# A fourth prepared half tile in the joint phase, with the forget gate kept in DRAM and one head pair moved behind the phase

## The chip, the cores and the metric

The kernel runs on one core of one Trainium2 chip. The metric is the device time of one execution in microseconds. TensorE (PE) multiplies, VectorE (DVE) and ScalarE (ACT) do elementwise work, GpSimd (POOL) and SyncE (SP) mostly issue DMAs. SBUF is the memory on the chip, PSUM holds the products, DRAM is outside.

## The reference

One layer of a hybrid decoder, 256 tokens of 2048 features, all in float32:

```python
h = rmsnorm(x, pre_norm_g[l])
proj = h @ w_in[l]
(a_q, a_k, a_v, a_g, a_lr, b_q, b_k, b_v, b_g, m_a, m_b) = jnp.split(proj, offsets, axis=-1)
gk = jax.nn.log_sigmoid((a_lr @ gla_gk_w2[l] + gla_gk_b[l])) / 16
o_a = gla_chunked(a_q, a_k, a_v, gk)             # gated linear attention, 4 heads
y_a = (rmsnorm(o_a, gla_norm_g[l]) * jax.nn.silu(a_g)) @ w_branch_a[l]
o_b = diff_attention(b_q, b_k, b_v, lam)         # differential attention, 16 heads
y_b = (rmsnorm(o_b, diff_norm_g[l]) * 0.8 * jax.nn.silu(b_g)) @ w_branch_b[l]
out = (jax.nn.sigmoid(m_a) * y_a + jax.nn.sigmoid(m_b) * y_b) @ w_out[l]
x = x + rmsnorm(out, post_norm_g[l])
```

`gk`, the log of the forget gate, is a 256 x 1024 array. It is made early, from the 16 columns `a_lr`, and read only when the scores of the gated linear attention are computed.

## The kernel before

**Half tiles.** Every weight matrix is streamed from DRAM once. Its unit is a half tile of 128 x 1024 elements. `emit_half` (L339) splits the next one of the list `seq` into a rounded high part (`hi`, written by ACT, L371) and a low part (`lo`, what is left, written by DVE, L372); TensorE then multiplies both with the split activations. `take` (L380) hands half tile j to the product that needs it, and before that calls `emit_half` until half tile j + `AHEAD` (3) is emitted. `hi` and `lo` lie in `wpool`, which has three buffers of each, so the conversion of half tile j + 3 starts when TensorE has finished half tile j.

**Stages.** First come the values of the linear attention (`v0`, `v2`, `v3`), while small tasks, among them `forget_gate` (L644), run beside them. Then comes the joint phase, described next. Behind it stand the remaining query and key heads of the differential attention (`diff_heads`), with the tasks of the attention scores (`gla_scores`, `gla_out`, `diff_lane`) in between, then the branch products, the output product and the final norm.

**The joint phase.** Ten sets of projection columns are multiplied with seven block products instead of eight (`PRODUCTS`, in the order 1, 3, 2, 5, 6, 7, 4). Each product has two tiles t of two half tiles h, so a set has 28 half tiles of six matmuls each. The operands of these products are sums and differences of weight blocks. Loads bring blocks a and b (`link`) and c (L242); DMAs that add while they write (L252, on POOL's queue) and additions on DVE (L260, in `follow_set`) turn them into the next operand in place. `phase_steps` (L102) writes the order out by hand. After both half tiles of a place listed in `PARTNERED` or `MORE_PARTNERS` it puts one half tile of other work, a partner: `v4`, the keys and queries of the linear attention, and the first `EARLY` (3) pairs of heads. A partner has 16 matmuls. Ten sets with six partners and four more make 64 partners. `pinned` keeps the matmuls of the phase in exactly this order.

**Buffers.** The pool behind `u` (L158) has `BIG` = 18 buffers of 128 x 1024. The activations hold eight of them all through the phase, and the forget gate `gp` two. The rest serve the c blocks, the gates `gl` and `gr` that each set makes, and the gathered `q` and `k`. Those are stored to DRAM by `spill` (L174) and come back by `fetch` (L180), both on POOL's queue in program order; in the last set the steps at (7, 1, 0) fetch `q` and `k` of both halves for `gla_scores`, which reads `gp` as `pre` (L948, L967).

**Pace.** Outside the phase, `tick` (L541) counts half tiles and advances the first three score tasks each time `PACE` half tiles have gone by: 1.5 in the stretch of heads ("linear"), 1.75 later.

Of the kernel before, what the change touches and what calls it, by code (L numbers as in the profile page):

```python
# [7 lines left out]
F32R = mybir.dt.float32r  # L8
# [6 lines left out]
P = 128  # L15
# [6 lines left out]
VG = (416, 416, 416, 416, 400)  # L22
RANK = 16
AHEAD = 3
LANES = 3
X_LOADS = {0: (2, 2), 1: (4, 4), 2: (8, 4), 3: (12, 4)}
ROWS = {"two": 2, "tok": 4, "chan": KT}
# [6 lines left out]
LINKS = {(3, 1): ("a", 0), (2, 0): ("a", 1), (7, 1): ("b", 0), (4, 0): ("b", 1)}  # L34
RAWS_AT = ((4, 1, 0), (2, 0, 1), (5, 1, 0))
PAIRS = [(g, pair) for g in range(4) for pair in range(2)]
EARLY = 3
PARTNERED = ((2, 1), (5, 1), (6, 0), (6, 1), (7, 0), (7, 1))
MORE_PARTNERS = ((0, 1, 0), (0, 1, 1), (0, 3, 1), (0, 5, 0))
SPILL_AT = (3, 0, 0)  # L40
PACE = {"linear": 1.5, "pairs": 1.75}
BIG = 18
MORE = 16
BRIDGE = 512
# [57 lines left out]
def phase_steps():  # L102

    keys = ["v4"] + [f"{name}{hf}{c}" for hf in range(2) for name in ("k", "q") for c in range(4)]
    keys += [f"{name}{g}{c}" for g, pair in PAIRS[:EARLY] for name in ("dq", "dk") for c in (2 * pair, 2 * pair + 1)]
    other = [(key, r, h) for key in keys for r in range(4 if key == "v4" else 1) for h in range(2)]
    slots = [(s, prod, t) for s in range(SETS) for prod in PRODUCTS for t in range(2)]
    mixed = []
    for slot in slots:
        mixed += [("set", *slot, h) for h in range(2)]  # L110
        s, prod, t = slot
        for _ in range(((prod, t) in PARTNERED) + (slot in MORE_PARTNERS)):
            mixed.append(other.pop(0))
    return mixed + other

# [27 lines left out]
def hybrid_kernel(ctx: ExitStack, tc, xt, xn, preg, postg, w, w2, gkb, glag, lamv, diffg, ident_d, causal_d, lmask_d, out):  # L143
# [14 lines left out]
    def u(shape, name, dtype=F32):  # L158
        count[0] += 1
        return big.tile(shape, dtype, tag="u", name=f"{name}_{count[0]}")  # L160
# [13 lines left out]
    def spill(t, name):  # L174
        count[0] += 1
        d = dram.tile(list(t.shape), t.dtype, name=f"{name}_{count[0]}")
        tc.keep_in_program_order(pool.dma_start(d, t))
        return d

    def fetch(d, name, make, queue=pool):  # L180
        t = make(list(d.shape), name, d.dtype)
        tc.keep_in_program_order(queue.dma_start(t, d))
        return t
# [23 lines left out]
    seq = halves_of("v0", "v2", "v3") + phase_steps()  # L207
# [3 lines left out]
    emitted = [0]  # L211
# [114 lines left out]

    loaded = [0]
    joint_loads = [False]
    alive = [0]

    def load_next(done):
# [7 lines left out]
    def emit_half():  # L339
        j = emitted[0]  # L340
        emitted[0] += 1
        e = seq[j]
        while loaded[0] < min(j + 2, len(seq)):
            if len(seq[loaded[0]]) == 3 and seq[loaded[0]][2] == 0:
                load(loaded[0])
            loaded[0] += 1
        joined = e[0] == "set"
        for link_ in part_links.get(e, ()):
            part_link(*link_)
        if e[0] == "part":  # L350
            r = chain[e[1], {3: "b", 7: "f"}.get(e[2], "e"), e[3]]
        else:
            r = emit_set(*e[1:]) if joined else emit_plain(j, *e)
        n = r.shape[1]
        if e[0] in ("o2", "o3") and j + 1 < len(seq):
            make = u if e == ("o3", 1, 0) else u2
            hi_t, lo_t = make([P, 1024], "keep", F32R), make([P, 1024], "keep", F32R)
        else:
            hi_t = wpool.tile([P, 1024], F32R, tag="hi", name=f"hi_{j}")
            lo_t = wpool.tile([P, 1024], F32R, tag="lo", name=f"lo_{j}")  # L360
        fine = 2 if j < 2 else 1
        cuts = [(n * i // fine, n * (i + 1) // fine) for i in range(fine)]
        if j == 0:
            prep_x(0)
            a, b = cuts[0]
            tc.keep_in_program_order(dve.tensor_copy(hi_t[:, a:b], r[:, a:b]))
            a, b = cuts[1]
            tc.keep_in_program_order(act.activation(hi_t[:, a:b], r[:, a:b], AF.Copy))
        for a, b in cuts:
            if j:  # L370
                act.activation(hi_t[:, a:b], r[:, a:b], AF.Copy)  # L371
            dve.tensor_tensor(out=lo_t[:, a:b], in0=r[:, a:b], in1=f32(hi_t[:, a:b]), op=ALU.subtract)  # L372
        if joined:
            follow_set(*e[1:])
        part_follow(e)
        ready[j] = (e, hi_t, lo_t)
# [3 lines left out]
    def take(key):  # L380
        j = used[0]
        used[0] += 1
        while emitted[0] < min(j + 1 + AHEAD, len(seq)):
            emit_half()
        e, hi, lo = ready.pop(j)
        assert key in (e, e[0]), (e, key)
        return hi, lo
# [130 lines left out]
    ts, heads = {}, {}  # L518
# [22 lines left out]
    def tick(part):  # L541
# [4 lines left out]
        if beat[0] > pace - 0.01:  # L546
            beat[0] -= pace
            pump(LANES)

# [94 lines left out]
    def forget_gate():  # L644
        w2_raw = w2_tile[0]
        w2_s = lend("s2l", "w2_s", F32R)
        top = lend("r3h", "w2h", F32R)
        r = slice(64, P)
        late = tc.keep_in_program_order
        late(act.activation(w2_s[:64, :], w2_raw[:64, :], AF.Copy))  # L650
        late(act.activation(top[r, :], w2_raw[r, :], AF.Copy))
        late(dve.tensor_tensor(out=w2_s[r, :], in0=w2_raw[r, :], in1=f32(top[r, :]), op=ALU.subtract))
        yield
        bank = ps("bg")
        for b in range(2):
            pe.transpose(bank[:, P * b : P * b + P], lr[:, b, :], ident)
        top = t2([P, 512], "lrh").bitcast(F32R)
        lrt = sm([P, S], "lrt", F32R, bufs=1)
        act.activation(top[:, :S], bank[:, :S], AF.Copy)
        for i in (0, 64):  # L660
            act.activation(lrt[i : i + 32, :], bank[i : i + 32, :S], AF.Copy)
            r = slice(i + 32, i + 64)
            dve.tensor_tensor(out=lrt[r, :], in0=bank[r, :S], in1=f32(top[r, :S]), op=ALU.subtract)
        yield
        gp.extend(u([P, 2, 4, P], "gp") for _ in range(2))
        for hf in range(2):
            for c in range(2):
                bank = ps("bg")
                for i in range(2):
                    ct = 4 * hf + 2 * c + i  # L670
                    o = bank[:, S * i : S * i + S]
                    pe.matmul(o, w2_s[:, P * ct : P * ct + P], lrt, start=True, stop=True)
                for i in range(2):
                    ct = 4 * hf + 2 * c + i
                    act.activation(gp[hf][:, :, 2 * c + i, :], bank[:, S * i : S * i + S].rearrange("p (b t) -> p b t", b=2), AF.Identity, bias=gkb_s[:, ct : ct + 1])
            yield
        e = [lend(tag, "e") for tag in ("r3h", "r3l")]
        z = [t.rearrange("p b c t -> p (b c t)") for t in gp]
        for hf in range(2):
            act.activation(e[hf], z[hf], AF.Abs)  # L680
            yield
            act.activation(e[hf], e[hf], AF.Exp, scale=-1.0)
            yield
        for hf in range(2):
            act.activation(e[hf], e[hf], AF.Ln, bias=1.0)
            yield
            dve.scalar_tensor_tensor(out=z[hf], in0=z[hf], scalar=0.0, in1=e[hf], op0=ALU.min, op1=ALU.subtract)
        done.add("gate")

    gp = []  # L690
# [229 lines left out]
    sets = (step for s in range(SETS) for step in block_products(s))  # L920
    rest = others()
    pinned[0] = joint_loads[0] = True
    fetched = []
    for n, step in enumerate(phase_steps()):
        if n == PUT_OFF:
            put_off.pop()()
        if step == ("set", SETS - 1, 7, 1, 0):
            fetched = [[fetch(ts[name, hf], name, u) for name in ("q", "k")] for hf in range(2)]
        next(sets if step[0] == "set" else rest)
    for gen in (sets, rest):  # L930
        assert next(gen, DONE) is DONE
    pinned[0] = joint_loads[0] = False
    joint.close()
    more = ctx.enter_context(tc.tile_pool(name="more", bufs=MORE))
    pools[:] = ctx.enter_context(tc.tile_pool(name="small", bufs=2)), more
# [390 lines left out]
    while "out" not in done:  # L1326
        pump(LANES)
    parts_a = []
# [7 lines left out]
    for g in range(4):  # L1336
        parts_a.append(fetch(m0[g], "part", u))
        banks = token_major(f"y0{g}", 512, a_ops, LANES, 4 if g == 3 else 8)
        if g < 3:
# [4 lines left out]
    def settle(q):  # L1344
        while not {("pair", q // 2, pair) for pair in range(2)} <= done:
            pump(LANES)

# [93 lines left out]
    def half_operand(ops, to, prod, kt):  # L1441
# [4 lines left out]
        while name not in to:  # L1446
            pump(LANES)
        return [t[:, kt, :] for t in to[name]]
# [93 lines left out]
    for n, step in enumerate(branch_steps()):  # L1542
# [3 lines left out]
        if n % 3 == 2 or {"lane0", "lane1"} <= done:  # L1546
            pump(LANES if len(tasks) > 1 else 1)
    pinned[0] = False
# [27 lines left out]
    for g in (2, 3):  # L1576
# [7 lines left out]
        if g == 2:  # L1584
            total(0, 2, bank, 2)
            for b in range(2):
                xres.append([])
                for i in range(2):
                    t = u([P, 1024], "xres")
# [3 lines left out]
    t = total(0, 3, bank)  # L1593
# [10 lines left out]
    for c in range(2):  # L1604
        bank = held["x"][:, 256:] if c else ps("mm")[:, :256]
        for kt in range(8, KT):
            lo = 512 * (kt % 2) + 256 * c
# [3 lines left out]
        if c == 0:  # L1611
            t = cell(1, 3)[:, :256]
# [4 lines left out]
        else:  # L1617
            end = ps("bg")
            c = slice(TURNED[0] % 1024, TURNED[0] % 1024 + 512)
            t = yg[1, 1][:, c]  # L1620
# [67 lines left out]
```

## Time and profile before

| | |
|---|---|
| median of 3 runs | 1079.25 us (1079.2 to 1079.81) |
| profiled execution | 1080.03 us |
| its span in the profile | 1078.1 us |
| PE busy | 1066.4 us (99%) |
| weight loads busy | 914.4 us (85%) |
| DVE busy | 959.7 us (89%) |
| ACT busy | 765.3 us (71%) |
| POOL busy | 179.6 us (17%) |
| DMA | 295.54 MB, mean 274 GB/s |
| joint phase | about 84 to 639 us |

Matmuls overlap, so the busy time of PE is longer than the sum of their pitches would be; the distance between the starts of successive matmuls says whether TensorE runs at its rate. A row of the timeline has start, length, engine, line, operation, output and inputs, the count of merged instructions, and in brackets the idle time of the engine before it with what ended it. A row of the waits has total, count and longest.

### The profile page before, as it was taken

To read this page: it belongs to the slowest core of one execution; us is meant where nothing else is said; L and a number is where in the kernel's file an instruction comes from. 1 tells how busy PE (TensorE), PEld (TensorE's weight loads), DVE (VectorE), ACT (ScalarE), POOL (GpSimd) and SP (SyncE) were. 2 spreads that over 40 slices of the span, in tenths; PEclk is the share of its full clock that TensorE was granted. 3 is DMA by queue.
4 is the path that set the end of the run, shared out by engine and by line. 5 is a ranking of instruction groups with operands and counts; after the bars stand their busy time and mean duration, and the time that the engine had idled before them with its cause. 6 is when DMAs were issued, how large, how long until landed. Compare 5 with 4: busy or idle time off the path is not lost.

```text
span 1078.1 us, 15451 instructions
## 1 busy us (share of the span) xinstructions
PE 1066.4 (99%) x5380; PEld 914.4 (85%) x5380; DVE 959.7 (89%) x1273; ACT 765.3 (71%) x1122; POOL 179.6 (17%) x259
## 2 busy tenths in 40 slices
PE   9999999999999999999999999999999999999997
PEld 8998888888888888888888888898988888888886
DVE  7798999999999999999999989976877988889886
ACT  7897676777676767676767766765687887566662
POOL 0201121212121212121212211012111112100000
PEclk9999999999999999999999999999999999999999
DMA  9899798989898989999898867769989888988752
GB/s 349 271 352 310 194 339 259 322 230 320 224 324 215 310 245 335 284 273 303 267 298 262 206 231 279 253 206 310 334 282 305 264 269 273 346 303 257 271 192 99
DMA packets 68365, 295.54 MB, mean 274 GB/s; under 512 B 8832, under 2 KB 11904, under 8 KB 51648
## 3 DMA queue, kind: packets, MB, share of 16 engines
q1 hardware_dynamic: 38080, 167.99, 43.8%
q0 software_dynamic: 29632, 125.84, 42.6%
q8 instruction: 42, 0.69, 0.3%
q10 hardware_dynamic: 576, 0.73, 0.2%
q14 instruction: 35, 0.29, 0.1%
HBM read 267.27 MB, written 27.26 MB: 273 GB/s over the span
## 4 chain that ended last, share of the span: by engine, by line
PE 82%; DVE 7%; issue 5%; ACT 2%; DMA 2%; POOL 1%; POOLq 0%; SPq 0%; DVEq 0%; ACTq 0%
PE mm L579 55%; PE bg L579 20%; DVE lo L372 3%; PE mm L567 2%; PE bg L567 2%; DMA vback<-vl 1%; PE mm L552 1%; DVE a L260 1%; ACT prob L1158 1%; ACT hi L371 1%; DMA raw<-in_w_dram 0%; DVE prob L1152 0%; PE bg L1172 0%; PE bg L1064 0%; PE bg L1364 0%
## 5 line engine op out<-in xcount | busy, mean ns | idle before, releaser
L371 ACT ACTIVATE hi<-raw 128x1024 fp32r<-128x1024 f32 (+3 forms) x213 | 217.0, 1025 | 117.0 <-PE bg L579 51.7
L372 DVE TENSOR_TENSOR lo<-raw,hi 128x1024 fp32r<-128x1024 f32 (+3 forms) x215 | 251.8, 1177 | 39.7 <-ACT hi L371 36.8
L371 ACT ACTIVATE hi<-a 128x1024 fp32r<-128x1024 f32 x160 | 169.3, 1061 | 53.7 <-PE mm L579 35.3
L372 DVE TENSOR_TENSOR lo<-a,hi 128x1024 fp32r<-128x1024 f32 x160 | 190.6, 1220 | 6.3 <-ACT hi L371 4.4
L579 PE MATMUL mm<-hi,xs 128*128 128x512 f32 (+1 forms) x608 | 155.8, 382 | 0.0
L579 PEld LDWEIGHTS mm<-hi,xs 128*128 128x128 f32 x608 | 114.0, 188 | 18.5
L579 PE MATMUL bg<-xs,hi 128*128 128x512 f32 x448 | 115.4, 390 | 0.0
L372 DVE TENSOR_TENSOR lo<-b,hi 128x1024 fp32r<-128x1024 f32 x80 | 97.8, 1223 | 12.3 <-ACT hi L371 9.9
L579 PEld LDWEIGHTS bg<-xs,hi 128*128 128x128 f32 x448 | 84.2, 188 | 16.4
L371 ACT ACTIVATE hi<-b 128x1024 fp32r<-128x1024 f32 x80 | 84.2, 1059 | 19.2 <-PE mm L579 17.3
L579 PE MATMUL mm<-lo,xs 128*128 128x512 f32 (+1 forms) x304 | 88.6, 381 | 0.0
L579 PE MATMUL mm<-xs,hi 128*128 128x512 f32 x320 | 82.2, 394 | 0.0
L252 POOL DMA_DIRECT2D b<-in_w_dram x40 | 34.9, 873 | 204.7 <-DVE a L260 123.1
L579 PEld LDWEIGHTS bg<-xs,lo 128*128 128x128 f32 x448 | 60.9, 190 | 6.9 <-DVE lo L372 2.8
L579 PEld LDWEIGHTS mm<-xs,hi 128*128 128x128 f32 x320 | 57.4, 189 | 9.9
L579 PEld LDWEIGHTS mm<-lo,xs 128*128 128x128 f32 x304 | 57.0, 188 | 9.7
L579 PE MATMUL bg<-xs,lo 128*128 128x256 f32 x448 | 62.8, 283 | 1.5 <-DVE lo L372 1.5
L372 DVE TENSOR_TENSOR lo<-c,hi 128x1024 fp32r<-128x1024 f32 x40 | 49.0, 1226 | 5.5 <-ACT hi L371 1.4
L579 PE MATMUL mm<-hi,oah 128*128 128x512 f32 x128 | 50.9, 397 | 1.3 <-DVE part L1334 1.3
L371 ACT ACTIVATE hi<-c 128x1024 fp32r<-128x1024 f32 x40 | 42.5, 1062 | 11.8 <-PE mm L579 10.9
L579 PE MATMUL mm<-hi,oal 128*128 128x512 f32 x128 | 50.1, 391 | 0.0
L260 DVE TENSOR_TENSOR a<-a,b 128x1024 f32<-128x1024 f32 x40 | 48.8, 1221 | 0.6
(408 smaller groups left out, 2283.9 us busy)
## 6 DMA issues: line engine op xcount, KB each, us to landing
raw<-in_w_dram SPq DMA_DIRECT2D x90, 1024.0 KB, 7.6
c<-in_w_dram SPq DMA_DIRECT2D x40, 512.0 KB, 6.9
a<-in_w_dram POOLq DMA_DIRECT2D x40, 512.0 KB, 9.5
b<-in_w_dram POOLq DMA_DIRECT2D x40, 512.0 KB, 8.3
a<-in_w_dram POOLq DMA_DIRECT2D x18, 1024.0 KB, 15.9
b<-in_w_dram POOLq DMA_DIRECT2D x18, 1024.0 KB, 9.8
raw<-in_w_dram SPq DMA_DIRECT2D x14, 832.0 KB, 7.8
gr<-gr POOLq DMA_DIRECT2D x10, 512.0 KB, 13.3
```

Source lines behind the costliest of these rows:

```text
L252: tc.keep_in_program_order(pool.dma_start(chain[s, name, i][:, c], block(s, 1, i)[:, c], accum_op=ALU.add))
L260: add = dve.tensor_tensor(out=a, in0=a, in1=chain[s, "b", i][:, c] if second else raws[s, i, h], op=ALU.add)
L371: act.activation(hi_t[:, a:b], r[:, a:b], AF.Copy)
L372: dve.tensor_tensor(out=lo_t[:, a:b], in0=r[:, a:b], in1=f32(hi_t[:, a:b]), op=ALU.subtract)
L552: i = pe.matmul(out, lhs, rhs, start=first and n == 0, stop=last and n == len(pairs) - 1, **kw)
L567: i = pe.matmul(banks[g][b][:, :n], a[part][:, P * b : P * b + P], w[:, n * g : n * g + n], start=first, stop=last)
L579: i = pe.matmul(*args, **kw)
L1158: act.activation(prob[m][:, lo:up], prob[m][:, lo:up], AF.Exp, scale=score_scale[:, b : b + 1], bias=mx[:, i : i + 1], accum_out=z[:, i : ...
```

## The change

In the joint phase `take` emits four half tiles ahead instead of three (`PHASE_AHEAD`). The buffers for every fourth half tile of the phase come from the pool of `u`, two each time, and the other three keep using `wpool`. `forget_gate` stores its two tiles to DRAM when it ends, and the last set fetches them back, each behind the `q` and `k` of its half. In the eight sets of `LEAN` the partner behind the second tile of product 2 is left out. The partners are then 56, and `EARLY` is 2: the third pair of heads is computed behind the phase, as one of six pairs there instead of five. The pace of the score tasks in the stretch of heads goes from 1.5 to 1.75 half tiles.

```diff
+PHASE_AHEAD = 4
...
-EARLY = 3
+EARLY = 2
 PARTNERED = ((2, 1), (5, 1), (6, 0), (6, 1), (7, 0), (7, 1))
 MORE_PARTNERS = ((0, 1, 0), (0, 1, 1), (0, 3, 1), (0, 5, 0))
+LEAN = (1, 2, 3, 4, 6, 7, 8, 9)
 SPILL_AT = (3, 0, 0)
-PACE = {"linear": 1.5, "pairs": 1.75}
+PACE = {"linear": 1.75, "pairs": 1.75}
...
-        for _ in range(((prod, t) in PARTNERED) + (slot in MORE_PARTNERS)):
+        for _ in range(((prod, t) in PARTNERED[s in LEAN :]) + (slot in MORE_PARTNERS)):
             mixed.append(other.pop(0))
...
+    joined_stage = [0]
...
+        elif joined_stage[0] and (j - joined_stage[0]) % 4 == 3:
+            hi_t, lo_t = u([P, 1024], "hi", F32R), u([P, 1024], "lo", F32R)
         else:
             hi_t = wpool.tile([P, 1024], F32R, tag="hi", name=f"hi_{j}")
...
-        while emitted[0] < min(j + 1 + AHEAD, len(seq)):
+        while emitted[0] < min(j + 1 + (PHASE_AHEAD if joined_stage[0] else AHEAD), len(seq)):
             emit_half()
...
+        gp[:] = [spill(t, "gp") for t in gp]
         done.add("gate")
...
     pinned[0] = joint_loads[0] = True
+    joined_stage[0] = emitted[0]
...
         if step == ("set", SETS - 1, 7, 1, 0):
-            fetched = [[fetch(ts[name, hf], name, u) for name in ("q", "k")] for hf in range(2)]
+            for hf in range(2):
+                fetched.append([fetch(ts[name, hf], name, u) for name in ("q", "k")])
+                gp[hf] = fetch(gp[hf], "gp", u)
...
     pinned[0] = joint_loads[0] = False
+    joined_stage[0] = 0
```

## The prediction

> **What bounds the kernel now.** I read the engine totals of the page first, then the chain in order of time for the rate of TensorE, then the windows set by set, and last the timelines around the few places where a set is longer than its neighbours.
>
> ```profile
> PE 1066.4 (99%) x5380; PEld 914.4 (85%) x5380; DVE 959.7 (89%) x1273; ACT 765.3 (71%) x1122; POOL 179.6 (17%) x259
> ```
> ```profile
> 138.82 21.78 PE mm L579 x96
> 160.60 2.77 PE bg L579 x16
> ```
> ```profile
> 138.82:193.66 54.84, 54.84 (x266) 46.30 (x265) 52.49 (x52) 39.91 (x43) 10.28 (x14) 1.00 0.94 301
> ...
> 413.02:468.45 55.43, 55.10 (x266) 46.21 (x265) 52.56 (x50) 40.37 (x44) 11.89 (x17) 1.00 0.97 299
> ...
> 523.29:579.05 55.76, 55.10 (x266) 46.22 (x265) 53.56 (x53) 40.79 (x45) 12.55 (x18) 1.00 0.89 263
> ```
> ```profile
> PE bg L579 <- DVE lo L372: 1.5, 3, 0.7
> ```
>
> In the joint phase TensorE runs without a gap: 96 matmuls in 21.78 us are 0.227 us each, so a set's half tile (six of them) takes 1.36 us and a partner's half tile (one row of 16) 2.77 us. A set is 28 of the first and six of the second, 54.84 us (the windows' columns are length, then PE, PEld, DVE, ACT, POOL, clock, DMA share, GB/s). The clock is 1.00 throughout. So the sets that last 55.43 and 55.76 show the loss: 0.59 us in set 6 and 0.92 us in set 8, and the chain of waits says what it is: TensorE stood three times for a low part that VectorE (DVE) had not finished. Set 0 has the third place:
>
> ```profile
> 133.92 0.39 PE L579 MATMUL mm<-hi,r3l 128*128 128x512 f32 x1
> 134.51 0.73 PE L579 MATMUL mm<-lo,r3h 128*128 128x512 f32 x2 [0.20 <-DVE lo L372]
> 135.08 1.78 PE L579 MATMUL bg<-xs,hi 128*128 128x512 f32 x7
> 137.38 1.21 PE L579 MATMUL bg<-xs,lo 128*128 128x256 f32 x8 [0.52 <-DVE lo L372]
> ```
>
> At a pitch of 0.227 the second row was due at 134.15 (0.36 late) and the fourth at 135.08 + 7 x 0.227 = 136.67 (0.71 late): 1.07 us. All that can be won in the phase is therefore 1.07 + 0.59 + 0.92 = 2.58 us, of 1078.1.
>
> **Lookahead, three to four half tiles.** How far DVE is ahead is read by pairing its low parts with the matmuls that first use them, here in set 8.
>
> ```profile
> 537.59 5.31 DVE L372 TENSOR_TENSOR lo<-c,hi 128x1024 fp32r<-128x1024 f32 x4
> ...
> 544.39 1.23 DVE L372 TENSOR_TENSOR lo<-a,hi 128x1024 fp32r<-128x1024 f32 x1
> ...
> 549.19 2.36 DVE L372 TENSOR_TENSOR lo<-a,hi 128x1024 fp32r<-128x1024 f32 x2
> ```
> ```profile
> 544.46 0.62 PE L579 MATMUL mm<-lo,xs 128*128 128x512 f32 x2
> ...
> 548.61 0.62 PE L579 MATMUL mm<-lo,r1h 128*128 128x512 f32 x2
> ...
> 551.33 0.61 PE L579 MATMUL mm<-lo,r1h 128*128 128x512 f32 x2
> ```
>
> The low part that ends at 537.59 + 5.31 = 542.90 is used at 544.46: a lead of 1.56 us. It does not grow in the run of 16 set half tiles, because the next conversion must wait for a buffer. At the first half tile of product 5 the lead is 548.61 - 545.62 = 2.99, since the partner that follows product 2 has put 2.77 us of TensorE work there instead of 1.36. Then the additions of L260 come, and two half tiles later the lead is 0.92 (the pair at 549.19 ends at 551.55, the first of it one pitch of 2.36 - 1.22 = 1.14 earlier, at 550.41). One buffer more adds one half tile, 1.36, to the lead wherever the buffer is what holds DVE back: 2.92 in the run, which is long enough for it: DVE gains 1.36 - 1.14 = 0.22 us on each half tile, 3.5 on 16. Later in each second half of a set it also waits for a buffer, and that idle time is what a fourth buffer lets it use:
>
> ```profile
> 123.60 1.23 DVE L372 TENSOR_TENSOR lo<-b,hi 128x1024 fp32r<-128x1024 f32 x1 [0.86 <-ACT hi L371]
> ```
> ```profile
> 453.38 1.22 DVE L372 TENSOR_TENSOR lo<-b,hi 128x1024 fp32r<-128x1024 f32 x1 [0.66 <-ACT hi L371]
> ```
> ```profile
> 563.65 1.22 DVE L372 TENSOR_TENSOR lo<-b,hi 128x1024 fp32r<-128x1024 f32 x1 [0.62 <-ACT hi L371]
> ```
>
> Set 0 can use 0.86 and the lead it carries in, against 1.07 lost: I take 1.0. Set 6 has 0.66 against 0.59: all of it. Set 8 has 0.62 against 0.92, and it loses a partner's evacuation besides: 0.8. Sum **-2.4 us**; the ends are 0 (DVE gets no earlier) and -2.6.
>
> **Eight sets without the partner of product 2.** Each lean set has 54.84 - 2.77 = 52.07 us of TensorE work. DVE loses one low part (1.14) and about 0.3 of evacuation, so of its idle 54.84 - 52.49 = 2.35 us about 1.05 is left: still less than TensorE's work. The lead at product 5 is then 2.92 from the fourth buffer where it was 2.99 from the partner: -0.07, so **0** by itself, as long as the fourth buffer is there. Without it the lead starts at 1.56, and the same additions, which took 2.99 - 0.92 = 2.07, would stop TensorE for 0.51 in each of eight sets: 4.1 us, the upper end.
>
> **The third early pair after the phase.** Eight half tiles leave the phase (8 x 2.77 = 22.2 us) and come back in the stretch that follows, where two half tiles take 650.11 - 644.52 = 5.59:
>
> ```profile
> 644.52 2.23 PE L579 MATMUL mm<-xs,hi 128*128 128x512 f32 x9
> ...
> 650.11 2.23 PE L579 MATMUL mm<-xs,hi 128*128 128x512 f32 x9
> ```
> ```profile
> 634.00:745.00 111.00, 110.90 (x662) 98.19 (x661) 95.57 (x145) 71.96 (x114) 20.85 (x38) 1.00 0.74 258
> ```
>
> 8 x 2.80 = 22.4, **+0.2**. TensorE is full in that stretch too (110.90 of 111), so nothing is filled up. Its weight loads, head stores and later fetches move with it, into a DMA share of 0.74 from one of 0.94.
>
> **Pace 1.75 instead of 1.5.** Five pairs are 40 half tiles, 40 / 1.5 = 26.7 steps of the score tasks; six are 48 / 1.75 = 27.4. The tasks end at the same place against the branch products, with more time a step. **0**, but where a DVE step then falls against the branch products is open: one bank there now comes late,
>
> ```profile
> 871.79 0.50 PE L579 MATMUL mm<-hi,oah 128*128 128x512 f32 x1 [0.83 <-DVE part L1334]
> ```
>
> and a shift can remove such a stop or make another: -1 to +1.
>
> **Forget gate stored and fetched.** Two stores and two fetches of 512 KB on POOL's queue.
>
> ```profile
> L687 DVE SCALAR_TENSOR_TENSOR gp<-gp,e x2: 1219/1222/1224, 69.7 to 72.9; 128x1024 f32<-128x1024 f32 x2
> L967 ACT ACTIVATE decay<-gp x2: 1044/1052/1059, 649.2 to 650.1; 128x1024 f32<-128x1024 f32 x2
> ```
> ```profile
> 79.92 0.91 POOL L252 DMA_DIRECT2D a<-in_w_dram  x1 [11.32 <-DVE lo L372]
> ```
>
> The gate is ready at 74 and POOL sits idle for 11.32 us up to 79.92, so the stores issue in that gap; what is behind them waits for DVE anyway. The fetches stand in POOL's queue among those of q and k, behind which only the last head and gate stores and gate fetches wait; the gate's reader comes at 649, some 25 us after. **0**; if the cover goes, one transfer of about 10 us would hold the score tasks, not TensorE, which has six pairs of head products to run. DVE's waits are unchanged by it.
>
> **Who holds the eighteen big buffers.** Storing the gate frees two, the fourth half tile takes two. The pool was full before: the queue of SP waits in it.
>
> ```profile
> SPq L242 <- DVE a L260: 166.3, 24, 22.9
> SPq L242 <- DMA gl<-gl: 113.3, 7, 29.6
> ```
> ```profile
> gl<-gl POOLq DMA_DIRECT2D x10, 512.0 KB, 14.0
> ```
>
> Loads waited here, off the path. Now a conversion on ScalarE (ACT) can wait in the same pool, with every later half tile behind it on ACT, DVE behind ACT and TensorE behind DVE. The trace of before cannot show that wait. Its ends are 0, if the pair always takes over the buffers its predecessor frees, and, if it has to wait for a store in flight, 14.0 less a lead of 2.9, 11 us each time. Below zero it cannot go, since the gain of the buffer is booked above. I take 0: the count of two for two is the nearer row, and SP's loads are ordered later in the program than the conversions that would need the buffer.
>
> **Sum.** -2.4 + 0 + 0.2 + 0 + 0 + 0, about -2.3 to -2.4. Against the profiled execution (1080.03 us, its span 1078.1 and 1.9 around it) that is 1077.7; the runs' median is 0.78 below that execution, so **1076.9**.
>
> **Rivals.** *The forecast, 0.50*: the three stops of the phase go, 1075.4 to 1077.1 with what the branch products do.
> *Little comes of it, 0.30*: half of the stops go (set 0 keeps its own, because its evacuations of v4 follow one another), or the branch products get one more stop of 1 us: 1079.25 - 1.2 = 1078.0. For it: DVE at 52 of 55 us gives little room; against it: the idle rows above.
> *The fourth pair comes late, 0.14, slower*: its buffer is held by a load or a store in flight, so the lookahead is three again in lean sets that have lost their partner's cushion: eight times 0.51 is 4.1, 1079.25 + 4.1 = **1083.3**. With the stops of the phase gone as forecast, it decides from 2.4 + 2.2 = 4.6 us of such waits: half a microsecond in each of nine sets, or a single whole flight of a store. For it: SP's 113.3 us; against it: the count.
> *DVE becomes the bound of the lean sets, 0.06, slower*: if the 2.35 us that DVE idles in a set cannot be used, a lean set lasts 54.84 - 1.44 = 53.40 instead of 52.07, 1.33 x 8 = 10.6, **1089.9**. Against it: undisturbed sets last 54.84, which is TensorE's sum (28 x 1.36 + 6 x 2.77), and DVE's 52.49 is less; hence the small chance.
> The Trainium skill, Perfetto Trace Analysis, Identifying the Most-Contended Engine, says that matmul busy time is a bad measure, and to judge TensorE by how busy its weight loads are. By that rule TensorE's 85% stands below DVE's 89%, DVE would be the engine to relieve, taking TensorE work from beside it would not shorten a set, and the time would be the last rival's; the even pitch of 0.227 us in this trace does not agree with the rule.
>
> **How the numbers follow.** From no change a measurement of this kernel can tell about 0.2%, 2.2 us: below 1077.1 is faster, above 1081.4 slower. The forecast's case gives 0.50, the second 0.30 same, the last two 0.20. The likeliest case alone is 1075.4 to 1077.1. For 8 in 10 the range runs from 1075.0 (all 2.6 us and a stop of the branch products gone) to 1083.3.
>
> **What would show it.** Right: all lean sets at 52.07 in the windows, no wait of TensorE for a low part between 84 and 612, the lead at product 5 near 2.9, the phase shorter by 22.2 + 2.4. Wrong: ACT's conversions waiting for a DMA of gl, gr or k; sets of 52.6 and more; a lead of 1.5 at product 5; new stops of the branch products by DVE; the gate's fetch ending the wait of L967.

## The result, and the profile after

| | before | after |
|---|---|---|
| median | 1079.22 us (1079.0 to 1079.81) | 1131.7 us (1128.29 to 1134.95) |
| ratio after to before | | 1.0487 [1.0463, 1.0511] |
| profiled execution, span | 1080.03, 1078.1 us | 1134.95, 1133.1 us |

The change makes the kernel 4.9% slower, where 1076.9 us had been predicted. First the engine totals of the page, and then the joint phase as one window of each kernel (columns: length, then busy time and instructions of PE, PEld, DVE, ACT, POOL, granted clock, DMA share, GB/s); before first, from its first half tile to its last:

```profile
PE 1085.5 (96%) x5380; PEld 921.4 (81%) x5380; DVE 953.1 (84%) x1273; ACT 752.8 (66%) x1122; POOL 179.8 (16%) x263
```
```profile
91.20:630.70 539.50, 537.79 (x2584) 454.27 (x2584) 513.76 (x488) 393.35 (x426) 105.72 (x148) 1.00 0.92 277
```
```profile
91.20:659.90 568.70, 532.55 (x2457) 441.82 (x2456) 493.56 (x472) 371.00 (x412) 104.31 (x145) 0.97 0.86 253
```

TensorE, DVE and ACT execute as many instructions as before. The phase has 127 matmul records fewer, since a pair of heads left it, and takes 29.2 us longer. TensorE is now idle for 36 us of it, and the clock is 0.97. The waits of TensorE in the phase (columns: total, times, longest):

```profile
PE mm L584 <- DVE lo L377: 21.8, 9, 7.4
PE mm L584 <- ACT hi L376: 6.3, 5, 5.0
PE mm L584 <- DVE gr L907: 4.8, 4, 2.6
```

(L376 and L377 are the old L371 and L372, L584 is L579.) What DVE and ACT waited for, in two views of the same stretch:

```profile
DVE lo L377 <- DMA gr<-gr: 29.2, 4, 9.4
DVE lo L377 <- DMA gl<-gl: 5.7, 1, 5.7
```
```profile
ACT hi L376 <- DMA gr<-gr: 8.3, 2, 6.0
```

A conversion reads no `gr`. What it waited for is the buffer: its tile was to lie where the gate of the previous set still lay, and that gate's store was in flight. One such place, on POOL, DVE, ACT and PE in turn:

```profile
381.56 0.85 POOL L179 DMA_DIRECT2D gr<-gr  x1
```
```profile
398.45 1.23 DVE L377 TENSOR_TENSOR lo<-raw,hi 128x1024 fp32r<-128x1024 f32 x1 [9.42 <-DMA gr<-gr]
```
```profile
400.89 1.06 ACT L376 ACTIVATE hi<-a 128x1024 fp32r<-128x1024 f32 x1 [7.68 <-DVE lo L377]
```
```profile
392.40 1.07 PE L584 MATMUL mm<-hi,xs 128*128 128x512 f32 x4
400.86 1.22 PE L584 MATMUL mm<-lo,xs 128*128 128x512 f32 x2 [7.39 <-DVE lo L377]
401.88 3.58 PE L584 MATMUL bg<-xs,hi 128*128 128x512 f32 x8
```

POOL issues the store at 381.56. It lands 16.8 us later, at 398.4, and DVE starts its low part at that moment, after 9.42 idle. DVE's low parts run in program order, so the ones behind it wait too. Those that are ready are used up by then: TensorE stands for 7.39 us, and ACT for 7.68, until DVE gives a buffer back. The five waits of DVE for gates are five stops of TensorE. Each ends 2.1 to 2.5 us after the `gr` of its set has landed, which is the time of two conversions, the one that waited for the buffer and the one behind it. (Late means: the distance of the two starts, less the usual pitch.)

| TensorE last started at | next start late by | `gr`, `gl` landed at |
|---|---|---|
| 221.46 us | 2.34 us | 221.5, 222.8 us |
| 276.95 | 5.90 | 280.6, 281.5 |
| 393.08 | 7.55 | 398.4, 399.5 |
| 457.65 | 4.62 | 460.0, 461.2 |
| 621.02 | 5.20 | 624.3, 625.6 |

Together 25.6 us. Six smaller stops (3.06 at 96.4, 2.73 at 129.3, four of 0.8 to 1.2) are for the most part a late load and late gate additions of L907. The matmuls behind a long stop are slow as well:

```profile
393.00:401.00 8.00, 0.61 (x4) 0.18 (x2) 2.55 (x3) 0.32 (x2) 0.00 (x0) 0.84 0.97 395
401.00:405.50 4.50, 4.50 (x12) 3.53 (x13) 4.47 (x5) 2.59 (x4) 0.90 (x1) 0.52 0.20 20
405.50:412.00 6.50, 6.50 (x34) 5.50 (x33) 5.76 (x6) 4.33 (x5) 1.31 (x2) 1.00 0.72 120
```

For 4.5 us after the stop the granted clock is 0.52, and the eight matmuls at 401.88 have a pitch of (405.29 - 401.88) / 8 = 0.426 us instead of 0.227. Added up over the starts of successive matmuls, this costs 11 us in the phase beyond the stops.

The other side of the exchange is SP's queue, in the same stretch:

```profile
SPq L244 <- DVE a L262: 340.2, 14, 54.8
SPq L244 <- DVE lo L377: 94.6, 3, 46.1
```

Before, the loads of c waited for the stores of `gl` and `gr`, off the path. Now no load does: loads take the buffers that the conversions and additions release, and the conversions are left with those under a store.

### The profile page after: what moved, and what is told of

It reads as the page before. It is cut to its first block, busy times and chain, and to the rows that moved or that the text cites. A ratio compares the mean times of both kernels' runs of the same rounds, so it can differ in the third digit from the quotient of the medians.

```text
span 1133.1 us, 15366 instructions
## 1 busy us (share of the span) xinstructions
PE 1085.5 (96%) x5380; PEld 921.4 (81%) x5380; DVE 953.1 (84%) x1273; ACT 752.8 (66%) x1122; POOL 179.8 (16%) x263
## 5 line engine op out<-in xcount | busy, mean ns | idle before, releaser
L377 DVE TENSOR_TENSOR lo<-raw,hi 128x1024 fp32r<-128x1024 f32 (+3 forms) x215 | 251.8, 1179 | 57.0 <-ACT hi L376 43.2
L376 ACT ACTIVATE hi<-raw 128x1024 fp32r<-128x1024 f32 (+3 forms) x213 | 215.4, 1022 | 89.1 <-PE mm L584 49.8
L376 ACT ACTIVATE hi<-a 128x1024 fp32r<-128x1024 f32 x160 | 165.2, 1055 | 110.7 <-PE mm L584 33.6
L377 DVE TENSOR_TENSOR lo<-a,hi 128x1024 fp32r<-128x1024 f32 x160 | 190.2, 1220 | 42.4 <-DMA gr<-gr 19.7
L584 PE MATMUL mm<-hi,xs 128*128 128x512 f32 (+1 forms) x608 | 158.2, 386 | 6.8 <-ACT hi L376 6.3
L584 PEld LDWEIGHTS mm<-hi,xs 128*128 128x128 f32 x608 | 114.2, 190 | 28.1 <-ACT hi L376 8.4
L584 PE MATMUL mm<-lo,xs 128*128 128x512 f32 (+1 forms) x304 | 91.0, 389 | 19.5 <-DVE lo L377 19.4
L377 DVE TENSOR_TENSOR lo<-b,hi 128x1024 fp32r<-128x1024 f32 x80 | 96.2, 1221 | 12.4 <-ACT hi L376 11.0
L376 ACT ACTIVATE hi<-b 128x1024 fp32r<-128x1024 f32 x80 | 83.2, 1053 | 35.1 <-PE mm L584 12.8
L584 PE MATMUL bg<-xs,hi 128*128 128x512 f32 x384 | 100.5, 394 | 0.0
L584 PE MATMUL mm<-xs,hi 128*128 128x512 f32 x384 | 98.0, 394 | 0.0
L584 PEld LDWEIGHTS bg<-xs,hi 128*128 128x128 f32 x384 | 73.3, 191 | 14.5
L584 PEld LDWEIGHTS mm<-lo,xs 128*128 128x128 f32 x304 | 56.9, 190 | 32.6 <-DVE lo L377 23.6
L584 PEld LDWEIGHTS mm<-xs,hi 128*128 128x128 f32 x384 | 69.1, 189 | 12.2
L584 PEld LDWEIGHTS bg<-xs,lo 128*128 128x128 f32 x384 | 52.5, 191 | 4.3 <-DVE lo L377 0.5
L584 PE MATMUL mm<-xs,lo 128*128 128x256 f32 x384 | 55.2, 283 | 0.0
L584 PEld LDWEIGHTS mm<-xs,lo 128*128 128x128 f32 x384 | 52.1, 190 | 3.3
L584 PE MATMUL bg<-xs,lo 128*128 128x256 f32 x384 | 53.6, 282 | 0.1
L377 DVE TENSOR_TENSOR lo<-c,hi 128x1024 fp32r<-128x1024 f32 x40 | 47.6, 1220 | 4.9 <-ACT hi L376 4.7
L584 PE MATMUL mm<-hi,oah 128*128 128x512 f32 x128 | 50.7, 396 | 0.2 <-DVE ob_copy L1243 0.2
L254 POOL DMA_DIRECT2D a<-in_w_dram x40 | 35.2, 1011 | 96.3 <-DVE lo L377 95.6
```

The costliest lines, as they stand in the source:

```text
L254: tc.keep_in_program_order(pool.dma_start(chain[s, name, i][:, c], block(s, 1, i)[:, c], accum_op=ALU.add))
L584: i = pe.matmul(*args, **kw)
```

## The experiments

The theory (A in some expectations) is the pool: the fourth pair of `hi` and `lo` comes from buffers that gates in flight still hold. Its rivals are the lean sets, in which TensorE overtakes DVE without the partner of product 2 (B), a pool that is too small by two buffers, whoever holds them (C), and the stored gate, whose stores and fetches cost the time. Fifteen kernels ran; the ratio is always to the kernel before on the same chip.

| kernel | us | ratio |
|---|---|---|
| `store_alone` | 1081.2 | 1.0016 [1.0006, 1.0025] |
| `lean_alone` | 1086.74 | 1.0064 [1.0051, 1.0076] |
| `no_fourth` | 1086.1 | 1.0057 [1.0045, 1.007] |
| `fourth_alone` | 1121.31 | 1.0383 [1.0365, 1.04] |
| `fixed_pair` | 1163.65 | 1.0776 [1.0758, 1.0794] |
| `fixed_no_lean` | 1124.94 | 1.0422 [1.0405, 1.0439] |
| `early_store` | 1137.62 | 1.0534 [1.0519, 1.0549] |
| `own_pair16` | 1086.05 | 1.0057 [1.0045, 1.007] |
| `own_pair_no_lean16` | 1084.28 | 1.0035 [1.0024, 1.0047] |
| `before16` | 1177.14 | 1.0885 [1.0849, 1.0922] |
| `in_place` | 1080.78 | 1.0003 [0.999, 1.0015] |
| `in_place_no_lean` | 1079.15 | 0.9993 [0.9979, 1.0008] |
| `xres_pair` | 1078.89 | 0.9996 [0.9988, 1.0005] |
| `xres_pair_pace` | 1078.36 | 0.9991 [0.9982, 1.0] |
| `xres_pair_no_lean` | 1077.75 | 0.9983 [0.9974, 0.9992] |

### Parts alone

`no_fourth` is the kernel after without the lookahead of four:

```diff
-PHASE_AHEAD = 4
+PHASE_AHEAD = 3
...
-        elif joined_stage[0] and (j - joined_stage[0]) % 4 == 3:
+        elif False:
```

> The changed kernel with a lookahead of three and no pair from the pool of u; gate in DRAM, lean sets, two early pairs and the pace stay. Theory A: no stop for a store in flight, but the lean sets lack the lead, about half a microsecond each: 1080 to 1084 us. Theory B: still 1120 us or more. Theory C: as A.

`fourth_alone` is the kernel after with the partners, early pairs and pace of before:

```diff
-EARLY = 2
+EARLY = 3
...
-LEAN = (1, 2, 3, 4, 6, 7, 8, 9)
+LEAN = ()
...
-PACE = {"linear": 1.75, "pairs": 1.75}
+PACE = {"linear": 1.5, "pairs": 1.75}
```

> The kernel before with the lookahead of four, its pair from the pool of u each time, and the gate in DRAM; all partners, three early pairs and the old pace are back. Theory A: the stops for gl and gr come without any lean set, 1110 to 1150 us. Theory B: no lean set, so about 1077 us. Theory C: as A.

`lean_alone` is `no_fourth` with the gate kept in its buffers:

```diff
-        gp[:] = [spill(t, "gp") for t in gp]
...
-                gp[hf] = fetch(gp[hf], "gp", u)
```

> The kernel before with the eight lean sets, two early pairs and the pace of 1.75; gate resident, lookahead three, no pair. no_fourth took 1086.1 with the gate stored besides. If the lean sets are what cost it, this takes 1085 to 1087 us too, with stops at the last partner of most sets; if the gate's store is, 1079 to 1081.

`store_alone` has both of the first two edits: of the change only the stored and fetched gate is left.

> The kernel before with the forget gate stored and fetched, nothing else. If the store is free as predicted: 1079 to 1080 us, the three stops of the phase still there. If it is what costs no_fourth its 6 us: 1084 to 1086.

The stored gate alone costs 0.16%, the lean sets with the moved pair and the pace 0.64%, both together 0.57%. The fourth half tile with the stored gate costs 3.83%, with every partner in its place. So the rivals give a few microseconds and the half tile some 40. The waits in the phase say the same. `fourth_alone`, TensorE and DVE:

```profile
PE mm L584 <- DVE lo L377: 23.0, 7, 7.6
```
```profile
DVE lo L377 <- DMA gr<-gr: 23.6, 3, 8.6
```

`no_fourth`, where no conversion waits for a DMA:

```profile
PE bg L584 <- DVE lo L377: 2.7, 6, 0.5
```

Five of these six stops are in lean sets, each at the last partner of its set, 0.3 to 0.5 us; the sixth, in set 0, was there before. The phase of `no_fourth` lasts 520.5 us. Before it was 539.5, of which 22.2 are the work that moved out (8 x 2.77), so the lean sets add 3.2 without the lookahead. The whole time lies 2 us above the 1080 to 1084 expected; 1.8 us are a wait of the attention scores behind the phase, for a fetched head (`qh`).

### One pair, reused

`fixed_pair` gives every fourth half tile the same two buffers, requested once when the phase starts; `fixed_no_lean` adds the edit of `fourth_alone`.

```diff
+    fourth = []
...
-            hi_t, lo_t = u([P, 1024], "hi", F32R), u([P, 1024], "lo", F32R)
+            hi_t, lo_t = fourth
...
+    fourth[:] = u([P, 1024], "hi", F32R), u([P, 1024], "lo", F32R)
```

> The changed kernel, but the fourth pair of hi and lo is taken from the pool of u once, at the start of the phase, and used again for every fourth half tile until its end. The pool has the same 18 buffers. Theory A (the pair asked for anew each time ends up in a buffer whose store of gl or gr is still in flight): the waits of DVE and ACT for gl and gr go, the phase loses its 44 us of stops and the 11 us of half-rate matmuls behind them, 1076 to 1079 us. Theory B (lean sets are bound by DVE): lean sets stay longer than 52.07 us, 1120 us or more. Theory C (the two buffers are simply too many for the pool, wherever they come from): gr, gl or the c blocks wait instead, 1090 to 1130 us.

> The kernel before with the gate in DRAM and a fourth pair taken once for the whole phase; all partners, three early pairs and the old pace. Theory A: the three stops of the phase (2.6 us) go, 1076 to 1078 us, and the difference to fixed_pair is what lean sets and the moved pair are worth. Theory B: faster than fixed_pair by 40 us. Theory C: 1090 us or more.

`emit_half` writes half tile j + 4 ahead of the product of half tile j in program order, so with one pair that product reads the data of half tile j + 4 and must wait for its conversion. These two therefore leave the products of every fourth half tile with other data, and the order of their waits is another: at 1163.65 and 1124.94 us they say nothing for or against the theory. A pool with one buffer, which hands a new tile out after the last reader of the old one, was needed instead.

### A pair of its own

The pair comes from a pool of one buffer per tag, and the pool of `u` has 16 buffers instead of 18, so the memory is the same. In `own_pair16` the new pool is opened last, behind `blocks` and `first`.

```diff
-BIG = 18
+BIG = 16
...
+    fourth = joint.enter_context(tc.tile_pool(name="fourth", bufs=1))
...
-            hi_t, lo_t = u([P, 1024], "hi", F32R), u([P, 1024], "lo", F32R)
+            hi_t = fourth.tile([P, 1024], F32R, tag="hi4", name=f"hi_{j}")
+            lo_t = fourth.tile([P, 1024], F32R, tag="lo4", name=f"lo_{j}")
```

> The changed kernel, but the fourth hi and lo have two buffers of their own beside the pool of u, which is cut from 18 to 16 buffers: the same memory, only that nothing else can take the pair's buffers. Theory A (a c load takes a buffer that the pair gave back, and the pair waits for a store in flight instead): no wait of DVE or ACT for gl or gr, no half-rate clock in the phase, 1076 to 1081 us (16 buffers of u instead of 18 may cost something outside the phase). Theory C (two buffers too few in the phase, whoever holds them): gl, gr or c wait instead, 1100 us or more.

The stops of the phase are gone: TensorE waits for nothing in it. 1131.7 us become 1086.05 with the same instructions and the same bytes of memory; only who may take which buffer differs. That shows the theory, and C, which had 1100 us or more, is out. But the time is 5 us above the 1076 to 1081 expected, because the matmuls of the phase are slower (below).

`early_store` tries the other way, to have the gates stored sooner:

```diff
-SPILL_AT = (3, 0, 0)
+SPILL_AT = (1, 0, 0)
```

> The changed kernel with the stores of gl and gr issued at product 1 of the next set instead of product 3 (SPILL_AT), 5.5 us earlier on TensorE's clock. Theory A: the pair waits for the same stores, which land some 5 us earlier, so stops of 4.6 to 7.6 us shrink to 0 to 3 and the half-rate stretches behind them mostly go: 1085 to 1105 us. Theory C: the buffers are held for 5 us less of every 52, the same direction but a few us only.

This missed: 1137.62 us, and DVE waits for `gr` as before. Both stores are issued together, and so not before the last half of `gl` is written. Kernel after, ACT and POOL, then the same in `early_store`:

```profile
261.38 0.67 ACT L874 ACTIVATE gl<-mm,rstd 128x512 f32<-128x512 f32 x1
```
```profile
264.22 1.29 POOL L179 DMA_DIRECT2D gr<-gr  x1
```
```profile
267.49 0.67 ACT L874 ACTIVATE gl<-mm,rstd 128x512 f32<-128x512 f32 x1
```
```profile
269.77 1.37 POOL L179 DMA_DIRECT2D gr<-gr  x1
```

Here the stores follow `gl` by 2.3 instead of 2.8 us, and the 11 to 15 us in flight stay. So the edit moved next to nothing. But `gr`, for which four of the five waits were, is finished much earlier. Kernel after, ACT and POOL:

```profile
254.06 0.73 ACT L866 ACTIVATE gr<-gr,minus_rstd 128x512 f32<-128x512 f32 x1 [2.18 <-DVE gr L916]
```
```profile
259.50 0.88 POOL L254 DMA_DIRECT2D a<-in_w_dram  x1 [8.65 <-DVE lo L377]
```

It is complete at 254.79 us, 9.4 us before its store is issued, and POOL stands idle for the first half of that time. A store of `gr` alone, directly behind product 7, could by these rows have started up to 9.4 us earlier; it wasn't tried.

### The pitch of the matmuls

In `own_pair16` the 120 matmuls between two partners take longer than in a kernel that has its pair elsewhere (`in_place`, next), with the granted clock at 1.00 in both. The chain of each, own pair behind `first`, then in place:

```profile
191.14 27.57 PE mm L586 x120
```
```profile
190.63 27.23 PE mm L586 x120
```

That is 0.2298 against 0.2269 us, and 519.7 against 514.8 us for the phase. The four kernels of the next group ask whether the place of the buffers does it. `before16`:

```diff
-BIG = 18
+BIG = 16
```

> The kernel before with 16 instead of 18 buffers in the pool behind u. Everything that is laid out behind this pool moves down by two buffers of 4 KB per partition, as it did in the kernel with a pair of its own. Theory (place): in that kernel the pitch of the set matmuls of high parts was 231 ns against 228 before because of where the buffers lie. Then the pitch is 231 here too and the phase takes 4 to 5 us more at its matmuls: 1083 to 1086 us. Rival (work): the pitch rose because ACT and DVE write more evenly beside a TensorE that doesn't stop. Then the pitch stays at 228 here. In both cases two buffers fewer can make loads of c late; if they do, TensorE's waits name the additions on a.

`in_place` opens the new pool directly behind the one of `u`, so that everything else lies where it lay:

```diff
     big = ctx.enter_context(tc.tile_pool(name="big", bufs=BIG))
+    fourth = ctx.enter_context(tc.tile_pool(name="fourth", bufs=1))
```

> The kernel after, with 16 buffers in the pool behind u and a pair of buffers of its own for every fourth half tile, laid out directly behind that pool, so that all that follows lies where it lay before and in the kernel after. Theory (place): the pitch of the set matmuls of high parts goes back from 231 to 228 ns, the phase is 4 to 5 us shorter than in the earlier kernel with a pair of its own (1086.05 us), and the time is 1080.5 to 1082.5 us. Rival (work): the pitch stays at 231 and the time at 1085 to 1087 us. Both: no stop of over 0.5 us in the phase.

`own_pair_no_lean16` and `in_place_no_lean` are `own_pair16` and `in_place` with the edit of `fourth_alone`.

> The earlier kernel with a pair of its own (1086.05 us), with all 64 partners, three early pairs and the pace of 1.5 kept as before: of the change only the fourth prepared half tile and the stored gate are left. The lean sets and the moved pair alone had cost 7.5 us, of which the stops at the last partners, 4 us, are gone already where a pair of its own is there. So both theories expect 3 to 4 us less than 1086.05: 1082 to 1083 us, with the pitch at 231 ns and no stop of over 0.5 us in the phase.

> All partners, three early pairs and the pace of 1.5 as before; the gate stored; the fourth half tile in a pair of buffers of its own, laid out directly behind the pool of u with 16 buffers. Theory (place): the pitch is 228 ns as before, the three stops of 2.5 us in all are gone from the phase, the stored gate costs 1 to 2 us: 1077.5 to 1079 us, the first version that is not slower than the kernel before. Rival (work): the pitch is 231 ns, and the time that of the same kernel with its pair laid out last, 1082 to 1083 us.

The kernels with a pair fell as the theory of the place had it: in place 1080.78 and 1079.15 us, behind `first` 1086.05, from which the theory was made, and 1084.28 (the two without lean sets a little above their ranges). The rival of the work is out: `in_place` has no stops either, and the old pitch. `before16` missed on both theories. Its pitch stayed at 228 ns in the undisturbed stretches although `blocks` and `first` lie where they lie in `own_pair16`. So their shift alone isn't the cause: either it is the place of the pair itself, or it needs a phase without stops. Which one is open; it wasn't tried.

`before16` shows something else, and 97 us of it. The longest pieces of one stretch of its chain, and TensorE's wait:

```profile
164.10 1.24 DVE lo L372
...
166.72 14.80 DMA gr<-gr
...
181.58 4.20 DMA c<-in_w_dram
```
```profile
PE mm L579 <- ACT hi L371: 51.3, 8, 10.5
```

With the gate still in it, a pool of 16 makes the load of c wait for the store of `gr`, and the conversion of c waits for the load. Before, the same waits of SP were harmless. The kernel before thus had fewer than two buffers to spare: its pool was full in the sense that counts, that with two buffers fewer a load on the path waits for a store.

In `in_place`, where the gate has freed two buffers and the pair has taken two, SP is back to waiting for stores as before, and no conversion waits for them:

```profile
SPq L245 <- DMA gl<-gl: 114.8, 6, 29.8
SPq L245 <- DMA gr<-gr: 53.6, 2, 27.9
```

### What was left after that

`in_place` is the change as it was forecast, with no conversion that waits for a store, and takes 1080.78 us where 1076.9 was forecast. The spans of its stages against before: the phase and the stretch of heads, up to the first branch product, 688.6 against 690.0, the output product 93.2 against 92.0, the tail 26.2 against 24.7. The tail (rows of PE, POOL, kernel `in_place`):

```profile
1057.06 0.50 PE L559 MATMUL mm<-keep,mh 128*128 128x512 f32 x1 [0.77 <-DVE keep L379]
```
```profile
1047.39 1.05 POOL L1602 DMA_DIRECT2D xres<-in_xn_dram  x2 [24.87 <-PE bg L586]
```

Two of the four loads of the residual `xres`, which take buffers of `u`, are issued at 1047 instead of about 1010 us, beside the last weight load, which then takes 6.9 us instead of 4.9. `xres_pair` gives them the pair's two buffers, idle by then; `xres_pair_no_lean` adds the edit of `fourth_alone`; `xres_pair_pace` is `xres_pair` with the pace of before.

```diff
-                    t = u([P, 1024], "xres")
+                    t = fourth.tile([P, 1024], F32, tag=("hi4", "lo4")[i], name=f"xres_{i}") if b else u([P, 1024], "xres")
```

> The whole change with the pair in place (1080.78 us), and the pair's two buffers used once more at the end, for the second row block of the residual xres. With 16 buffers in the pool of u these two loads were issued at 1047.4 and 1047.9 us, beside the last weight load, which took 6.9 us instead of 4.9; the tail took 26.2 us against 24.7 before. Theory (buffers): the loads start near 1010 us again, the last weight load takes 5 us, the tail is 24.7 us and the time 1079.0 to 1079.6 us. Rival (the moved pair delays the end): the tail stays at 26 us and the time at 1080.8 us. Both leave the 1.2 us lost in the output product.

> The same with all partners, three early pairs and the pace of 1.5 as before: of the change only the fourth prepared half tile and the stored gate are left (1079.15 us with the late loads). Theory (buffers): the tail goes from 26.1 to 24.7 us and the time to 1077.5 to 1078.0 us, 0.998 of the kernel before: the first version below it. Rival: 1079.2 us.

> The first kernel of this group with the pace in the stretch of heads back from 1.75 to 1.5 half tiles per step. Theory: the pace is worth nothing, as the prediction took it, and the time is that of the first kernel within 0.8 us. Rival: the 1.75 makes the score tasks late and causes the stops in the output product; then the time is 1.2 us lower, about 1078 us.

The pair's two loads no longer stand there, the last weight load takes 4.9 and 5.2 us, the tail 24.7 again, and the times are 1078.89 and 1077.75: the loss in the tail was the late loads. `xres_pair_no_lean` is the one version below the kernel before, by 0.17% [0.08, 0.26]. With the pace of 1.5 the output product loses nothing any more in the profiled execution (91.7 against 93.5 us), as the rival had it, and that is all of the 1.7 us between the two profiled executions. But the medians differ by 0.53 us, as the theory had it: the profiled execution of `xres_pair` is 1.2 us above its median. Two single profiles don't settle which holds.

## Why the prediction was wrong

**The step that failed** is "Who holds the eighteen big buffers". It took 0, with the words that "the count of two for two is the nearer row, and SP's loads are ordered later in the program than the conversions that would need the buffer". `in_place` shows that two for two suffices where nothing else may take the two. But a count doesn't say which tile gets which buffer at what time. The gate had held its two buffers for the whole phase; as part of the pool they went to any tile, and every fourth half tile asked anew for two, about eight times in a set. In five sets it had to wait for a buffer in which `gl` or `gr` of the set before lay, for 13 to 17 us under a store. The runs showed some 40 us in place of the 0 with all partners (`fourth_alone` 3.83% against 0.16% for the stored gate), and 51 us in the whole change (1131.7 against 1080.78 of `in_place`). One part of this stays open. The pair of half tile j + 4 is asked for in the program ahead of the product of half tile j, so in the common pool two pairs can be alive for a time, where the own pool allows one. How much comes from that second pair, and how much from other tiles taking the buffers, the runs don't separate.

**The price of the right rival.** "The fourth pair comes late", 0.14, had the mechanism: "its buffer is held by a load or a store in flight". Its price, 4.1 us, was that of a lookahead of three. But a late buffer doesn't take the lookahead back to three. `emit_half` runs in order, so DVE stops at that low part (in one of the five cases ACT at the high part), and the later conversions stand behind it, though the other three pairs could be filled. "Who holds the eighteen big buffers" had worked this out, "14.0 less a lead of 2.9, 11 us each time", as an upper end, and neither the rival's price nor the range used it. The measured rows are 2.3 to 7.55 us each time, five times, and TensorE's half clock behind the stops of the phase, 11 us, which no row of before could show.

**Lookahead, -2.4: right**, once the pair has its own buffers. The phase of `in_place_no_lean` is 537.1 us against 539.5, and no wait of TensorE is left in it.

**Lean sets, 52.07 us and a lead of 2.92 at product 5: right.** In `in_place`, a set, then the low part and the matmul that uses it:

```profile
190.63:242.69 52.06, 52.06 (x250) 43.87 (x249) 51.09 (x49) 39.30 (x42) 10.78 (x15) 1.00 0.90 259
```
```profile
524.09 1.23 DVE L379 TENSOR_TENSOR lo<-a,hi 128x1024 fp32r<-128x1024 f32 x1
```
```profile
528.24 0.62 PE L586 MATMUL mm<-lo,r1h 128*128 128x512 f32 x2
```

528.24 - 525.32 = 2.92. DVE is busy for 51.09 of these 52.06 us, so "DVE becomes the bound of the lean sets" falls too, and with it the rule that the prediction set beside it: by the Trainium skill, Perfetto Trace Analysis, Identifying the Most-Contended Engine, TensorE with weight loads of 43.87 us would stand far below DVE here (the page's other measure, the share of the peak rate, was not taken), yet the set lasts exactly as long as TensorE's work. Without the fourth buffer the prediction had 4.1 us for the lean sets, 0.51 in each of eight behind the additions at product 5; `no_fourth` shows 3.2, and its stops at the last partner of five sets. (The prediction's 28 x 1.36 + 6 x 2.77 is 54.7; the 54.84 is the window's. Nothing hangs on it.)

**The phase shorter by 22.2 + 2.4 = 24.6**: `in_place` 514.8 against 539.5, 24.7.

**The moved pair, +0.2, and the pace, 0: too low.** `xres_pair` against `xres_pair_no_lean` is 1.1 us together, of which the pace is about half by the medians. The prediction's -1 to +1 for the pace holds.

**The stored gate, 0**: `store_alone` shows 1.7 us [0.6, 2.7]. Its single profile is 1.9 us longer than before: 0.9 in the phase (540.4 against 539.5) and 1.0 in a wait of the branch products, before and then in `store_alone`:

```profile
PE mm L579 <- DVE part L1334: 1.3, 2, 0.8
```
```profile
PE mm L584 <- DVE part L1344: 2.3, 2, 1.5
```

That the store and its fetches cause both is not shown.

**What would show it wrong** named the row that then appeared, "ACT's conversions waiting for a DMA of gl, gr or k" (it was DVE's part of the conversion more than ACT's).

## What to carry to other kernels

A buffer pool that many kinds of tiles share is a queue: before giving one more of its buffers to work on the critical path, look for the longest time that any tile holds a buffer after its last write (here 9.4 us until the store of `gr` was issued and 13 to 17 us under it) and ask what of the critical path would stand behind it. Work of the bottleneck's feeder gets buffers of its own, where the same memory then costs nothing. And where a text of a prediction works out a price as the upper end, the rival and the range must use that price.

## What the runs showed of the hardware

TensorE's clock after a stop. Behind the stop of 2.34 us the granted clock was about half, and behind the one of 1.22 at 337.65 it stayed at 1.00. But it also stayed at 1.00 behind the stop of 3.06 at 96.4. The three, in order of time:

```profile
99.70:103.70 4.00, 3.98 (x20) 3.67 (x21) 3.31 (x3) 2.29 (x3) 0.00 (x0) 1.00 1.04 379
...
223.90:227.90 4.00, 3.87 (x10) 3.06 (x11) 4.00 (x5) 1.93 (x3) 0.00 (x0) 0.57 0.04 16
...
338.90:343.00 4.10, 3.90 (x17) 3.25 (x18) 4.07 (x5) 2.48 (x3) 0.00 (x0) 1.00 1.03 430
```

So the length of the stop alone doesn't decide. In the trace of the kernel after, the stretches at half rate in the phase start at 132.23, 224.39, 279.00, 398.47, 463.32 and 623.75 us. All of these are a whole number of 3.413 us apart, and each stretch lasts one, two or three times that. In the 3.413 us before these starts TensorE had been idle for 2.57, 2.18, 2.07, 3.41, 2.59 and 2.34 us. Before no other boundary of this grid at which the clock was still full had it been idle for more than 1.87 us: the stop at 96.4 lies across a boundary, with 1.27 us on one side and 1.63 on the other. The limit is not sharp, since the ends of matmuls are modelled; in `early_store` 1.73 us were enough.

The Trainium skill, TensorE: Matmul & The Clock Gate, Part 1, gives half rate as the idle state, entered after at least one idle window of about 3.4 us and left after about as long. The half rate, the 3.4 us and the pitch agree (its 426.7 ns for 512 columns, 426 here). But the window need not be idle throughout: here 2.07 us of it sufficed, so the measurement decides. A stop of two to three microseconds can cost more than itself, 1.7 us by the starts of the matmuls behind the one of 2.34.

The pitch of back-to-back matmuls depended on where the pair's pool of two buffers of 4 KB per partition lies: 0.2298 against 0.2269 us at a granted clock of 1.00, 4.9 us over the phase. The matmuls of high parts alone slowed, 0.231 against 0.228 us, those of low parts stayed at 0.227. Why is open.
